# Key buffers by whole head or fixed tile, and the head norm weights applied at the transposed copy, in a streaming encoder step

## The chip, the cores and the metric

One core of a Trainium2 chip runs one launch of the kernel. The metric is the device time of one execution in microseconds (us). The kernel before was timed three times: 1062.08 us in the median, from 1061.17 to 1062.24. The profile is of a separate execution.

## What is computed

The reference is one layer of a hybrid encoder on 1024 prompt rows and 64 sample rows (9 row tiles; the sample rows also see 256 cached rows). Everything is 32-bit floating point.

```python
proj = rms_norm(x) @ w_in                       # 1024 -> 5280 columns
a = softmax(q1 k1) - lam * softmax(q2 k2)       # differential attention, 4 heads
o_a = rms_norm(a @ v, da_head_norm_g) * (1.0 - lam_init)      # per head, 128 wide
o_b = softmax(q_m k_m) @ v_m                    # latent attention (MLA), 8 heads
y = x + (sigmoid(g_a) * ((o_a * silu(z_a)) @ w_branch_a)
         + sigmoid(g_b) * ((o_b * silu(z_b)) @ w_branch_b)) @ w_out
```

Both attentions are causal by chunks of 64 rows. The norm of a differential head is over the 128 columns of the head, so its weight is one number per column, and its factor one number per row.

## The kernel before

A product of two 32-bit operands is made of three matmuls: each operand is split into a rounded part and the rest (`split`, `split_ps`: ScalarE copies, GpSimd or VectorE subtracts), and `mm3` (L252 to L254) multiplies rounded by rounded, rounded by rest and rest by rounded.

The program runs in stages: the projections for the latent attention, then the latent attention (`mla_streams`), then the differential attention (`da_streams`), then the rest of the dense work, the branch products and the output product. Through both attentions a background stream (`dense`) gives TensorE the remaining columns of the input projection, 24 matmuls for one PSUM buffer; I call them dense matmuls. Their results are copied by ScalarE (L904) into `st` tiles (`stg`, 4 buffers) and stored to HBM.

TensorE's order is made by a planner in Python (`Order`): each stream is a generator that yields the time at which its next step can be ready, what it costs on TensorE and which buffers it takes (`Slots`), and the planner always takes the stream that can go on first. The order on the other engines and the order of the DMAs come from the Tile scheduler. PSUM has four one-bank buffers (`pj`), which transposes, attention products and dense work share, and two two-bank buffers for scores (`sc`).

**Latent attention.** `fetch` loads, for each head, keys in chunks of 512, 512 and 320 columns (raw tiles from `rawp`, 4 buffers of 512) and splits each into a tile of its own (`kp`, 4 buffers). `unit` takes one query tile t: scores against `128*(t+1)` keys, in chunks of 512 and the rest (L1004 to L1006), the maximum (VectorE L1012), the exponential (ScalarE L1015), the division by the sum (GpSimd L1017), the transposes (L1035). `out` multiplies by the values (L1073, L1074).

**Differential attention.** A key chunk is loaded by rows, transposed by TensorE (L1178) and written by `put_k` into a tile `K` of four planes: both key halves rounded, and their rests, which are zero in the other half's 64 partitions. GpSimd writes those zeros anew for each of the 12 chunks (L1174, L1175). The scores are L1233 and L1234, the mask L1236, the maximum L1238, the exponential L1240, the transposes L1261, the value products L1276 and L1278; the head's 9 output tiles collect in `oraw` (`H.o`) (L1283, L1284). After the ninth, VectorE works out the factor `fd` of each row (L1292 to L1297; the square root is ScalarE's and needs another function table there and back) and multiplies the 9 tiles by `fd` and the weights `gda`, which lie on all partitions:

```python
for t_ in range(NT):
    m = rows(t_)
    V.scalar_tensor_tensor(H.o[:m, t_], H.o[:m, t_], fd[:m, t_:t_ + 1], gda[:m], op0=ALU.mult, op1=ALU.mult)
```

Then `out` transposes them in groups of 4, 4 and 1 (L1311), ScalarE copies each group to the one tile `otT` (L1313), and a DMA stores it to `oT`, which the next stage loads again.

Of the kernel before, what the change touches and what calls it, by code (L numbers as in the profile page):

```python
# [11 lines left out]
F32 = mybir.dt.float32  # L12
# [8 lines left out]
P = 128  # L21
# [34 lines left out]
    (1, 1, S, 4, 128), (1, 1, S, 4, 128), (1, 1, S, 256), (1, 1, S, 32),  # L56
    (1, 1, SS, 4, 128), (1, 1, SS, 4, 128), (1, 1, SS, 256), (1, 1, SS, 32),
)


def rows(t):
# [3 lines left out]
def f32(ap):  # L65
    return ap.bitcast(F32)
# [105 lines left out]
def trunk(ctx: ExitStack, tc: tile.TileContext, i: dict, o: list):  # L172
# [751 lines left out]


    def mla_streams(fx):
        kp = pool(fx, "kp", 4)
        vp = pool(fx, "vp", 4)
        qp = pool(fx, "qp", 3)
        rawp = pool(fx, "rawp", 4)  # L930
        pcp = pool(fx, "pcp", 4)
        ptp = pool(fx, "ptp", 3)
        otp = pool(fx, "otp", 2)
        s_k, s_v, s_q, s_pc, s_pt = Slots(4), Slots(4), Slots(3), Slots(4), Slots(3)
        start = od.now + 16.0

        class Head:
# [9 lines left out]
        def fetch():  # L947
            for H in heads:
                h = H.h
                pr, e = h // 2, h % 2  # L950
                hs = slice(64 * e, 64 * e + 64)
                for what in (("k", 0), ("q", 0), ("q", 1), ("k", 1), ("q", 2), ("q", 3), ("k", 2), ("q", 4)):
                    c = what[1]
                    if what[0] == "k":
                        yield start, 0.0, [(s_k, 1), (s_v, 1)]
                        k0, n = (0, 512, S)[c], (512, 512, 320)[c]
                        raw = rawp.tile([P, 512], F32, name="raw")
                        load(raw[:MR, :n], mk[h, :, k0:k0 + n])
                        K = kp.tile([MR, 2, 512], F32R, name="K")
                        split(raw[:MR, :n], K[:, 0, :n], K[:, 1, :n])  # L960
                        H.K[c], H.tK[c] = K, t_split(od.on_dma(P * n * 4), n)
                        raw = rawp.tile([P, 512], F32, name="raw")
                        Vt = vp.tile([P, 4, 2, 64], F32R, name="V")
                        nb = 4 if c < 2 else 2
                        rv = raw[:, 0:256].rearrange("p (b d) -> p b d", d=64)
                        load(rv[:, :nb], mv[k0:k0 + nb * P, h * 64:(h + 1) * 64].rearrange("(b p) d -> p b d", p=P))
                        split(rv[:, :nb], Vt[:, :nb, 0], Vt[:, :nb, 1])
                        if c == 2:
                            load(rv[:SS, 2], mv[S + PAST:TK, h * 64:(h + 1) * 64])
                            split(rv[:SS, 2], Vt[:SS, 2, 0], Vt[:SS, 2, 1])  # L970
                        H.V[c], H.tV[c] = Vt, t_split(od.on_dma(130e3), 256)
                    else:
                        yield start, 0.0, [(s_q, 1)]
                        q0, nq = c * 256, 256 if c < 4 else 64
                        raw = rawp.tile([P, 512], F32, name="raw")
                        load(raw[:MR, :nq], mq[h, :, q0:q0 + nq])
                        Q = qp.tile([MR, 2, 256], F32R, name="Q")
                        split(raw[:MR, :nq], Q[:, 0, :nq], Q[:, 1, :nq])
                        H.Q[c], H.tQ[c] = Q, t_split(od.on_dma(P * nq * 4), nq)

        def unit(H, t):
# [2 lines left out]
            a0 = (t % 2) * P  # L984
            if t < 8:
                nk = P * (t + 1)
                chunks = [(c, min(512, nk - 512 * c)) for c in range((nk + 511) // 512)]
                msz = [P] * (t + 1)
            else:
                nk, chunks, msz = 320, [(2, 320)], [P, P, SS]  # L990

            def ready():
                if jc not in H.tQ or any(c not in H.tK for c, _ in chunks):
                    return None
                return max([H.tQ[jc]] + [H.tK[c] for c, _ in chunks])

            yield ready, sum(3 * c_mm(m) for _, m in chunks) + 0.03, [(s_sc, 1), (s_pc, 1)]
            sc = psc.tile([P, 1024], F32, name="sc")
            Q = H.Q[jc]
            for x_, (c, m) in enumerate(chunks):  # L1000
                dst = sc[:n, x_ * 512:x_ * 512 + m]
                qh, ql = Q[:, 0, a0:a0 + n], Q[:, 1, a0:a0 + n]
                kh, kl = H.K[c][:, 0, :m], H.K[c][:, 1, :m]
                TE.matmul(dst, qh, kh, start=True, stop=False)  # L1004
                TE.matmul(dst, qh, kl, start=False, stop=False)
                TE.matmul(dst, ql, kh, start=False, stop=True)  # L1006
            if t % 2 == 1 or t == 8:
                s_q.give(od.now)
            if t in (7, 8):
                s_k.give(od.now, 2 if t == 7 else 1)  # L1010
# [92 lines left out]


    def da_streams(fx):
        kp = pool(fx, "kpd", 4)
        vp = pool(fx, "vpd", 4)
        qp = pool(fx, "qpd", 3)
        rawp = pool(fx, "rawpd", 3)
        pcp = pool(fx, "pcpd", 4)  # L1110
        ptp = pool(fx, "ptpd", 4)
        otp = pool(fx, "otpd", 1)
        orp = pool(fx, "orp", 2)
        gda = orp.tile([P, P], F32, name="gda", bufs=1)
        load(gda, i["da_head_norm_g"][0].partition_broadcast(P))
        s_k, s_v, s_q, s_pc, s_pt, s_or = Slots(4), Slots(4), Slots(3), Slots(2), Slots(4), Slots(2)

        class Head:
            pass

        heads = []
        for h in range(DA_H):
# [22 lines left out]
        def fetch():  # L1145
            for H in heads:
                h = H.h
                for what in (("k", 0), ("q", 0), ("q", 1), ("k", 1), ("q", 2), ("q", 3), ("k", 2), ("q", 4)):
                    c = what[1]
                    if what[0] == "k":  # L1150
# [18 lines left out]
                            split(rv[:SS, 2], Vt[:SS, 2, 0], Vt[:SS, 2, 1])  # L1169
                        H.V[c], H.tV[c] = Vt, t_split(od.on_dma(512e3), 512)  # L1170
                        yield od.dma + 0.95, 0.11 * len(bl), [(s_tr, 1)]
                        K = kp.tile([P, 4, 512], F32R, name="K")

                        G.memset(f32(K[64:128, 2]), 0.0)  # L1174
                        G.memset(f32(K[0:64, 3]), 0.0)  # L1175
                        tr = ptr.tile([P, 512], F32, name="pj")
                        for b, m in enumerate(bl):
                            TE.transpose(tr[:, b * P:b * P + m], rk[:m, b], ident[:m, :m])  # L1178
# [23 lines left out]
        def unit(H, t):  # L1202
# [86 lines left out]
            if H.n == NT:  # L1289
# [222 lines left out]
```

## Time and profile before

| | us |
|---|---|
| median of three runs | 1062.08 |
| the profiled execution | 1064.11 |
| its span, first to last instruction | 1062.3 |
| TensorE busy in the span | 1027.8 |
| VectorE, ScalarE, GpSimd busy | 589.8, 557.3, 317.9 |

PE stands for TensorE's matmuls, PEld for its weight loads, DVE for VectorE, ACT for ScalarE, POOL for GpSimd, SP for SyncE, whose queue issues nearly all DMAs. A wait names the instruction whose end released the engine. Matmuls overlap in the pipeline, so a matmul's price is read from its start to the start of the next, not from its duration. The latent attention stands at about 250 to 518 us, the differential attention at about 530 to 800, the first branch product at 864.6.

### The profile page before, as it was taken

The page shows a single profiled execution, that of the slowest core. Times are in us where ns is not written, and L with a number is a line of the kernel's source. Part 1 is how long each engine was busy: PE and PEld are TensorE (multiplying, and loading weights), DVE is VectorE, ACT ScalarE, POOL GpSimd, SP SyncE. Part 2 cuts the span into 40 slices and gives each one's busy share as a digit, 9 for nine tenths or more (in the row PEclk, how much of TensorE's full clock was granted, in tenths as well). Part 3 has the DMA queues.
Part 4 walks back from the last instruction along what each step waited for, and adds up shares of the span by engine and source line. Part 5 has one row for each costly group of instructions (what it writes and reads, how often), then busy time and mean ns, then how long its engine had stood idle before and what let it go on. Part 6 is the DMA issues. An engine that isn't in the chain of part 4 may idle for free.

```text
span 1062.3 us, 18645 instructions
## 1 busy us (share of the span) xinstructions
PE 1027.8 (97%) x6391; PEld 971.0 (91%) x6391; DVE 589.8 (56%) x1396; ACT 557.3 (52%) x1411; POOL 317.9 (30%) x401
## 2 busy tenths in 40 slices
PE   5989999999999999999999989999999999999997
PEld 5989899999999999999999989899899999998885
DVE  5765833015566656665357767667754513564743
ACT  5554413335666666566456666666656554423422
POOL 3012202015545455444321222122103553512200
PEclk8999999999999999999999999999999999999999
DMA  6443556565323542332243232332218875531322
GB/s 214 125 103 70 130 133 181 177 159 157 100 82 96 138 112 68 95 93 76 74 119 99 60 110 69 98 96 65 74 50 264 255 250 180 171 103 50 110 80 80
DMA packets 154878, 126.64 MB, mean 119 GB/s; under 512 B 36960, under 2 KB 141792, under 8 KB 154784
## 3 DMA queue, kind: packets, MB, share of 16 engines
q1 hardware_dynamic: 153552, 123.22, 40.3%
q10 hardware_dynamic: 1232, 2.23, 0.6%
q8 instruction: 51, 0.84, 0.3%
q14 instruction: 43, 0.35, 0.1%
HBM read 80.50 MB, written 45.52 MB: 119 GB/s over the span
## 4 chain that ended last, share of the span: by engine, by line
PE 45%; DVE 2%; DMA 2%; ACT 2%; issue 1%; SPq 0%; POOL 0%; ACTq 0%
PE pj L252 12%; PE pj L254 11%; PE pj L253 11%; PE pj L1276 2%; PE sc L1233 2%; PE sc L1234 2%; PE pj L1261 2%; DMA oT<-otT 1%; PE pj L1278 1%; DVE oraw L1300 1%; DMA z<-zT 1%; SPq L190 0%; PE pj L1178 0%; PE pj L1196 0%; PE pj L1453 0%
## 5 line engine op out<-in xcount | busy, mean ns | idle before, releaser
L252 PE MATMUL pj<-hT,w 128*128 128x352 f32 (+1 forms) x576 | 199.7, 347 | 4.8 <-DVE ot L1080 1.3
L254 PE MATMUL pj<-hT,w 128*128 128x352 f32 (+1 forms) x576 | 188.3, 327 | 0.0
L253 PE MATMUL pj<-hT,w 128*128 128x352 f32 (+1 forms) x576 | 188.1, 327 | 0.0
L239 POOL TENSOR_TENSOR w<-wr,w 128x384 fp32r<-128x384 f32 (+3 forms) x81 | 74.3, 919 | 280.2 <-ACT w L238 238.8
L252 PE MATMUL pj<-w,hT 128*128 128x384 f32 (+1 forms) x384 | 133.1, 347 | 2.2 <-ACT krt L546 1.0
L253 PE MATMUL pj<-w,hT 128*128 128x384 f32 (+1 forms) x384 | 127.1, 331 | 0.6 <-POOL w L431 0.6
L254 PE MATMUL pj<-w,hT 128*128 128x384 f32 (+1 forms) x384 | 127.0, 331 | 0.3 <-DVE hT L243 0.3
L252 PEld LDWEIGHTS pj<-hT,w 128*128 128x128 f32 x576 | 108.8, 189 | 8.2 <-ACT otT L1313 1.7
L238 ACT ACTIVATE w<-wr 128x384 fp32r<-128x384 f32 (+3 forms) x161 | 73.6, 470 | 68.4 <-PE pj L254 32.4
L253 PEld LDWEIGHTS pj<-hT,w 128*128 128x128 f32 x576 | 108.8, 189 | 0.1
L254 PEld LDWEIGHTS pj<-hT,w 128*128 128x128 f32 x576 | 108.1, 188 | 0.0
L243 DVE TENSOR_TENSOR PT<-pj,PT 128x512 fp32r<-128x512 f32 (+4 forms) x168 | 83.8, 511 | 42.3 <-ACT PT L242 40.8
L239 DVE TENSOR_TENSOR w<-wr,w 128x384 fp32r<-128x384 f32 (+2 forms) x80 | 50.8, 635 | 78.5 <-ACT w L238 78.0
L242 ACT ACTIVATE PT<-pj 128x512 fp32r<-128x512 f32 (+4 forms) x168 | 72.9, 454 | 33.1 <-PE pj L1035 23.0
L252 PEld LDWEIGHTS pj<-w,hT 128*128 128x128 f32 x384 | 73.0, 190 | 4.5 <-ACT krt L546 1.3
L253 PEld LDWEIGHTS pj<-w,hT 128*128 128x128 f32 x384 | 73.1, 190 | 1.4 <-POOL w L431 0.9
L254 PEld LDWEIGHTS pj<-w,hT 128*128 128x128 f32 x384 | 72.7, 189 | 0.6 <-DVE hT L243 0.6
L1017 POOL TENSOR_SCALAR pc<-pc,zs 128x128 f32<-128x128 f32 (+8 forms) x72 | 52.3, 729 | 51.8 <-DVE zs L1016 50.4
L1240 ACT ACTIVATE pc<-sc,mx 128x128 f32<-128x128 f32 (+8 forms) x72 | 51.4, 716 | 28.9 <-DVE mx L1238 28.3
L1012 DVE TENSOR_REDUCE mx<-sc 128x1 f32<-128x128 f32 (+8 forms) x72 | 51.9, 722 | 21.3 <-PE sc L1006 20.4
L254 PE MATMUL pj<-u,w 128*128 128x352 f32 (+1 forms) x192 | 62.8, 327 | 0.0
L253 PE MATMUL pj<-u,w 128*128 128x352 f32 (+1 forms) x192 | 62.8, 327 | 0.0
(252 smaller groups left out, 2524.6 us busy)
## 6 DMA issues: line engine op xcount, KB each, us to landing
wr<-in_w_in SPq DMA_DIRECT2D x84, 192.0 KB
g<-gT SPq DMA_DIRECT2D x16, 544.0 KB
x<-in_x_prompt SPq DMA_DIRECT2D x15, 512.0 KB
dqkv<-st SPq DMA_DIRECT2D x32, 192.0 KB
gT<-st SPq DMA_DIRECT2D x32, 176.0 KB
z<-zT SPq DMA_DIRECT2D x8, 544.0 KB
o<-oT SPq DMA_DIRECT2D x8, 544.0 KB
out<-st SPq DMA_DIRECT2D x64, 64.0 KB
```

Of the source, the lines that this page charges most:

```text
L238: A.activation(hi, raw, AF.Copy)
L239: (eng or G).tensor_tensor(lo, raw, f32(hi), op=ALU.subtract)
L242: A.activation(hi, ps, AF.Copy)
L243: V.tensor_tensor(lo, ps, f32(hi), op=ALU.subtract)
L252: TE.matmul(ps, lh, rh, start=first, stop=False)
L253: TE.matmul(ps, lh, rl, start=False, stop=False)
L254: TE.matmul(ps, ll, rh, start=False, stop=last)
L1012: V.tensor_reduce(out=mx[:n], in_=sc[:n, :nk], op=ALU.max, axis=AX.X, negate=True)
L1017: G.tensor_scalar(pc[:n, :nk], pc[:n, :nk], zs[:n], 1.0, op0=ALU.mult, op1=ALU.mult)
L1233: TE.matmul(dst, qs, H.K[ch][:, c, :m], start=True, stop=False)
L1234: TE.matmul(dst, qs, H.K[ch][:, 2 + c, :m], start=False, stop=not masked)
L1240: A.activation(pc[:n, :nk], sc[:n, :nk], AF.Exp, bias=mx[:n], accum_out=H.z[:n, c, t:t + 1])
```

## The change

Line numbers above 58 are 8 higher after the change from a new function on, and up to 16 higher further down.

Latent attention: a head's 1024 prompt keys lie in one tile (two buffers), the 320 sample keys in another (`Ks`, one buffer). Query tile 4, with 640 keys, is scored in two chunks of 320 in place of 512 and 128; its PSUM columns begin at 192 so that each chunk stays in a bank. The raw tiles are two of 512 columns for keys and three of 256 for queries and values.

Differential attention: the four key tiles are fixed, and their zero parts are written once ahead of the stage, half by VectorE and half by GpSimd. The multiplication by `fd` is one GpSimd instruction for the 8 full tiles and one for the last. The weights are a column of one number per partition and go in as the scale of ScalarE's copy of the transposed output. The groups are 3, 3 and 3 tiles and the copy goes to an `st` tile; `otT` is gone.

```diff
+def key_chunks(nk):
+    if nk <= 512:
+        return [(0, nk)]
+    m = max(nk - 512, 512) if nk != 640 else 320
+    return [(0, m), (m, nk - m)]
...
     def mla_streams(fx):
-        kp = pool(fx, "kp", 4)
+        kp = pool(fx, "kp", 2)
-        rawp = pool(fx, "rawp", 4)
+        rawp = pool(fx, "rawp", 2)
...
-                        K = kp.tile([MR, 2, 512], F32R, name="K")
-                        split(raw[:MR, :n], K[:, 0, :n], K[:, 1, :n])
+                        if c == 0:
+                            H.K[0] = kp.tile([MR, 2, S], F32R, name="K")
+                        elif c == 2:
+                            H.K[1] = kp.tile([MR, 2, 320], F32R, name="Ks", bufs=1)
+                        K = H.K[c // 2][:, :, k0 % S:k0 % S + n]
+                        split(raw[:MR, :n], K[:, 0], K[:, 1])
-                        raw = rawp.tile([P, 512], F32, name="raw")
+                        raw = rawp.tile([P, 256], F32, name="raw2", bufs=3)
...
-                chunks = [(c, min(512, nk - 512 * c)) for c in range((nk + 511) // 512)]
+                ks, chunks, msz = (0, 1)[:(nk + 511) // 512], key_chunks(nk), [P] * (t + 1)
+            b0 = 512 - chunks[0][1] if len(chunks) == 2 else 0
...
-            sc = psc.tile([P, 1024], F32, name="sc")
+            sc = psc.tile([P, 1024], F32, name="sc")[:, b0:]
...
     def da_streams(fx):
-        otp = pool(fx, "otpd", 1)
-        gda = orp.tile([P, P], F32, name="gda", bufs=1)
-        load(gda, i["da_head_norm_g"][0].partition_broadcast(P))
+        gda = orp.tile([P, 1], F32, name="gda", bufs=1)
+        load(gda, i["da_head_norm_g"][0].rearrange("(p a) -> p a", a=1))
+        keys = [kp.tile([P, 4, 512], F32R, name=f"K{e}") for e in range(4)]
+        for K in keys:
+            V.memset(f32(K[64:128, 2]), 0.0)
+            G.memset(f32(K[0:64, 3]), 0.0)
...
-                        K = kp.tile([P, 4, 512], F32R, name="K")
-                        G.memset(f32(K[64:128, 2]), 0.0)
-                        G.memset(f32(K[0:64, 3]), 0.0)
+                        K = keys[(3 * h + c) % 4]
...
-                for t_ in range(NT):
-                    m = rows(t_)
-                    V.scalar_tensor_tensor(H.o[:m, t_], H.o[:m, t_], fd[:m, t_:t_ + 1], gda[:m], op0=ALU.mult, op1=ALU.mult)
-                H.to = od.on_dve(od.on_act(t2, 2500) + 1.0, 2300, 0.001)
+                for m, ts in ((P, slice(0, 8)), (SS, slice(8, 9))):
+                    o_ = H.o[:m, ts]
+                    G.tensor_tensor(o_, o_, fd[:m, ts].unsqueeze(2).broadcast_to(list(o_.shape)), op=ALU.mult)
+                H.to = od.on_pool(od.on_act(t2, 2500) + 2.0, 1152)
...
-            for t0 in (0, 4, 8):
-                ts = range(t0, min(t0 + 4, NT))
+            for t0 in (0, 3, 6):
+                ts = range(t0, t0 + 3)
...
-                ot = otp.tile([P, 512], F32, name="otT")
-                A.activation(ot[:, :w], tr[:, :w], AF.Copy)
+                ot = stg.tile([P, 384], F32, name="st")
+                A.activation(ot[:, :w], tr[:, :w], AF.Copy, scale=gda)
```

The planner's times shift with these lines, so TensorE's order differs from the first 640-key unit on, and with it the other engines' orders. Three places:

VectorE at the end of the first differential head, before, from the reciprocal of the next head's unit to that head's key chunk:

```order
L1249 RECIPROCAL f<-zda 128x1
L1300 SCALAR_TENSOR_TENSOR oraw<-oraw,fd,gda 128x128 x8
L1300 SCALAR_TENSOR_TENSOR oraw<-oraw,fd,gda 64x128
L1250 SCALAR_TENSOR_TENSOR f<-f,zda,neglam 128x1
L1284 TENSOR_TENSOR oraw<-pj,oraw 128x128
L243 TENSOR_TENSOR PT<-pj,PT 128x256
L1238 TENSOR_REDUCE mx<-sc 128x1 x2
L1252 SCALAR_TENSOR_TENSOR pc<-pc,f 128x384
L1133 TENSOR_TENSOR K<-pj,K 64x512
L1134 TENSOR_TENSOR K<-pj,K 64x512
```

The same place now, from the last step of the factor:

```order
L1312 SCALAR_TENSOR_TENSOR fd<-fd,r_7989 128x9
L1253 TENSOR_REDUCE mx<-sc 128x1
L1151 TENSOR_TENSOR K_7007<-pj,K_7007 64x512
L1152 TENSOR_TENSOR K_7007<-pj,K_7007 64x512
L1299 TENSOR_TENSOR oraw<-pj,oraw 128x128
L1253 TENSOR_REDUCE mx<-sc 128x1
L247 TENSOR_TENSOR w<-wr,w 128x256
```

The nine multiplications are gone from this queue, and the next head's key chunk (`K_7007` is the first of the four fixed tiles) stands two instructions behind the factor.

GpSimd between the two attentions, before:

```order
L1017 TENSOR_SCALAR pc<-pc,zs 128x1024
L1174 MEMSET K 64x512
L1175 MEMSET K 64x512
L1174 MEMSET K 64x512
L1175 MEMSET K 64x512
L1174 MEMSET K 64x512
L1175 MEMSET K 64x512
L1174 MEMSET K 64x512
L1175 MEMSET K 64x512
L1017 TENSOR_SCALAR pc<-pc,zs 64x320
```

And now:

```order
L1029 TENSOR_SCALAR pc<-pc,zs 128x896
L1137 MEMSET K_7007 64x512
L1137 MEMSET K_7008 64x512
L1137 MEMSET K_7009 64x512
L1137 MEMSET K_7010 64x512
L247 TENSOR_TENSOR w<-wr,w 128x256
L1029 TENSOR_SCALAR pc<-pc,zs 128x1024
L1029 TENSOR_SCALAR pc<-pc,zs 64x320
```

Four fills of zeros in place of eight stand ahead of the last division, but also ahead of the last but one, and a weight split has come between.

ScalarE at the first differential head's output copies, now:

```order
L1329 ACTIVATE st<-pj,gda 128x384
L1255 ACTIVATE pc,zda<-sc,mx 128x512
L246 ACTIVATE V<-raw 128x2x128
L1329 ACTIVATE st<-pj,gda 128x384
L246 ACTIVATE V<-raw 64x128
L912 ACTIVATE st<-pj 128x384
L1158 ACTIVATE Q<-pj 64x256
L1159 ACTIVATE Q<-pj 64x256
L1329 ACTIVATE st<-pj,gda 128x320
```

The three copies (L1329, before L1313) now share the four `st` buffers with the dense copies (L912, before L904); the value splits that wait for a DMA still stand among them.

## Rows read from the trace of the kernel before

**Rows 1.** The page, parts 1 and 2: busy time; granted clock in 40 slices.

```profile
PE 1027.8 (97%) x6391; PEld 971.0 (91%) x6391; DVE 589.8 (56%) x1396; ACT 557.3 (52%) x1411; POOL 317.9 (30%) x401
...
PEclk8999999999999999999999999999999999999999
```

**Rows 2.** Waits of TensorE, 500 to 830 us: total, times, longest.

```profile
PE pj L1196 <- issue: 1.9, 1, 1.9
PE pj L1035 <- POOL pc L1017: 1.3, 1, 1.3
PE pj L252 <- DVE K L1134: 1.2, 1, 1.2
PE pj L1196 <- ACT otT L1313: 1.2, 1, 1.2
PE pj L252 <- ACT otT L1313: 1.2, 2, 0.8
PE pj L252 <- DVE PT L243: 0.9, 1, 0.9
PE pj L1276 <- ACT otT L1313: 0.6, 1, 0.6
```

**Rows 3.** Timeline of TensorE at a 640-key and a 320-key unit: start, duration, instruction.

```profile
256.92 0.39 PE L1004 MATMUL sc<-K,Q 104*128 104x512 f32 x1
...
257.88 0.39 PE L252 MATMUL pj<-hT,w 128*128 128x384 f32 x1
...
271.69 0.31 PE L1004 MATMUL sc<-K,Q 104*64 104x320 f32 x1
...
272.13 0.32 PE L252 MATMUL pj<-hT,w 128*128 128x352 f32 x1
272.29 0.32 PE L253 MATMUL pj<-hT,w 128*128 128x352 f32 x1
```

**Rows 4.** Timeline of ScalarE at three head ends; in brackets the idle time before.

```profile
622.16 0.22 ACT L1313 ACTIVATE otT<-pj 128x64 f32<-128x64 f32 x1 [2.18 <-DMA oT<-otT]
...
682.12 0.42 ACT L238 ACTIVATE V<-raw 128x256 fp32r<-128x256 f32 x1 [2.58 <-DMA raw<-in_cache_da_v]
...
811.69 1.09 ACT L238 ACTIVATE u<-o 128x1088 fp32r<-128x1088 f32 x1
812.69 0.58 ACT L1313 ACTIVATE otT<-pj 128x512 f32<-128x512 f32 x1
```

**Rows 5.** Timeline of VectorE at the ends of the first and second head.

```profile
606.45 0.17 DVE L1297 SCALAR_TENSOR_TENSOR fd<-fd,r 128x9 f32<-128x9 f32 x1
...
608.03 2.42 DVE L1300 SCALAR_TENSOR_TENSOR oraw<-oraw,fd,gda 128x128 f32<-128x128 f32 x9
...
672.27 4.07 DVE L1300 SCALAR_TENSOR_TENSOR oraw<-oraw,fd,gda 128x128 f32<-128x128 f32 x9
...
677.42 0.69 DVE L1134 TENSOR_TENSOR K<-pj,K 64x512 fp32r<-64x512 f32 x1
```

**Rows 6.** Timeline of GpSimd and VectorE between the attentions.

```profile
511.89 0.52 POOL L1174 MEMSET K<- 64x512 f32 x1
...
515.82 0.52 POOL L1175 MEMSET K<- 64x512 f32 x1
516.33 0.53 POOL L1017 TENSOR_SCALAR pc<-pc,zs 64x320 f32<-64x320 f32 x1
...
516.06 0.43 DVE L1080 TENSOR_TENSOR ot<-pj,ot 64x256 f32<-64x256 f32 x1 [3.77 <-ACT ot L1079]
```

**Rows 7.** Groups by line, GpSimd's product of 1024 columns: busy, mean ns.

```profile
L239 POOL TENSOR_TENSOR ms<-mT,ms 128x1024 fp32r<-128x1024 f32 (+1 forms) x7 | 16.0, 2293 | 55.8 <-ACT ms L238 55.8
```

**Rows 8.** Timeline of TensorE: the first differential head's last value product.

```profile
600.63 0.22 PE L1278 MATMUL pj<-V,PT 64*64 64x128 f32 x1
```

**Rows 9.** Timeline of GpSimd beside VectorE's products of the second head.

```profile
673.39 1.15 POOL L239 TENSOR_TENSOR w<-wr,w 128x384 fp32r<-128x384 f32 x1 [7.11 <-ACT w L238]
674.63 0.62 POOL L1135 TENSOR_SCALAR K<-K 64x512 fp32r<-64x512 f32 x1
```

More of the change, by code (lines that the diff above doesn't have):

```diff
@@ L933, in mla_streams @@
         otp = pool(fx, "otp", 2)
-        s_k, s_v, s_q, s_pc, s_pt = Slots(4), Slots(4), Slots(3), Slots(4), Slots(3)
+        s_k, s_v, s_q, s_pc, s_pt = (Slots(2), Slots(1)), Slots(4), Slots(3), Slots(4), Slots(3)
         start = od.now + 16.0
@@ L954, in fetch @@
                     if what[0] == "k":
-                        yield start, 0.0, [(s_k, 1), (s_v, 1)]
+                        yield start, 0.0, [(s_k[c // 2], 1 - c % 2), (s_v, 1)]
                         k0, n = (0, 512, S)[c], (512, 512, 320)[c]
@@ L958, in fetch @@
                         load(raw[:MR, :n], mk[h, :, k0:k0 + n])
-                        K = kp.tile([MR, 2, 512], F32R, name="K")
-                        split(raw[:MR, :n], K[:, 0, :n], K[:, 1, :n])
-                        H.K[c], H.tK[c] = K, t_split(od.on_dma(P * n * 4), n)
-                        raw = rawp.tile([P, 512], F32, name="raw")
+                        if c == 0:
[4 more added lines that the diff above has]
+                        split(raw[:MR, :n], K[:, 0], K[:, 1])
+                        H.tK[c] = t_split(od.on_dma(P * n * 4), n)
+                        raw = rawp.tile([P, 256], F32, name="raw2", bufs=3)
                         Vt = vp.tile([P, 4, 2, 64], F32R, name="V")
                         nb = 4 if c < 2 else 2
-                        rv = raw[:, 0:256].rearrange("p (b d) -> p b d", d=64)
+                        rv = raw.rearrange("p (b d) -> p b d", d=64)
                         load(rv[:, :nb], mv[k0:k0 + nb * P, h * 64:(h + 1) * 64].rearrange("(b p) d -> p b d", p=P))
@@ L974, in fetch @@
                         q0, nq = c * 256, 256 if c < 4 else 64
-                        raw = rawp.tile([P, 512], F32, name="raw")
+                        raw = rawp.tile([P, 256], F32, name="raw2", bufs=3)
                         load(raw[:MR, :nq], mq[h, :, q0:q0 + nq])
@@ L986, in unit @@
                 nk = P * (t + 1)
-                chunks = [(c, min(512, nk - 512 * c)) for c in range((nk + 511) // 512)]
-                msz = [P] * (t + 1)
-            else:
-                nk, chunks, msz = 320, [(2, 320)], [P, P, SS]
+                ks, chunks, msz = (0, 1)[:(nk + 511) // 512], key_chunks(nk), [P] * (t + 1)
+            else:
+                nk, ks, chunks, msz = 320, (2,), [(0, 320)], [P, P, SS]
+            b0 = 512 - chunks[0][1] if len(chunks) == 2 else 0
             def ready():
-                if jc not in H.tQ or any(c not in H.tK for c, _ in chunks):
+                if jc not in H.tQ or any(c not in H.tK for c in ks):
                     return None
-                return max([H.tQ[jc]] + [H.tK[c] for c, _ in chunks])
+                return max([H.tQ[jc]] + [H.tK[c] for c in ks])
             yield ready, sum(3 * c_mm(m) for _, m in chunks) + 0.03, [(s_sc, 1), (s_pc, 1)]
-            sc = psc.tile([P, 1024], F32, name="sc")
-            Q = H.Q[jc]
-            for x_, (c, m) in enumerate(chunks):
-                dst = sc[:n, x_ * 512:x_ * 512 + m]
+            sc = psc.tile([P, 1024], F32, name="sc")[:, b0:]
+            Q, K = H.Q[jc], H.K[t // 8]
+            for c0, m in chunks:
+                dst = sc[:n, c0:c0 + m]
                 qh, ql = Q[:, 0, a0:a0 + n], Q[:, 1, a0:a0 + n]
-                kh, kl = H.K[c][:, 0, :m], H.K[c][:, 1, :m]
+                kh, kl = K[:, 0, c0:c0 + m], K[:, 1, c0:c0 + m]
                 TE.matmul(dst, qh, kh, start=True, stop=False)
@@ L1009, in unit @@
             if t in (7, 8):
-                s_k.give(od.now, 2 if t == 7 else 1)
+                s_k[t - 7].give(od.now)
             mx = small.tile([P, 1], F32, name="mx")
@@ L1105, in da_streams @@
     def da_streams(fx):
-        kp = pool(fx, "kpd", 4)
+        kp = pool(fx, "kpd", 1)
         vp = pool(fx, "vpd", 4)
```

## The prediction

> **What bounds the kernel now.** I read the page first. [...] There is no idle stretch in which an added matmul would be free, and none in which a removed wait is made up for elsewhere: dense work that TensorE gets done earlier in the attentions is not there any more behind them. A microsecond off TensorE's waits is therefore worth a microsecond of the end. A microsecond on another engine is worth nothing, unless TensorE comes to wait for it.
>
> So I read TensorE's waits next, from the last latent units to the last differential head [rows 2]. There are few, 8.3 us in the rows shown, and nearly all of them stand at four places that the change touches. To see what is behind each I took the timelines of ScalarE [rows 4], VectorE [rows 5] and GpSimd [rows 6] at those places. Durations are of the profiled execution, 1064.11 us, which is 2.03 above the median of the runs, 1062.08. I make the sum against 1064.11 and take the same number of microseconds from the median.
>
> **The change part by part.** *640 keys as 320 and 320.* The number of instructions on TensorE is the same before and after. Only these units change, one for each of 8 heads. With 512 and 128 columns the scores take from 256.92 to 257.88, 0.96 us; a 320-column pair takes from 271.69 to 272.13, 0.44, and two of them 0.88 [rows 3]. The saving is 0.08 x 8, **-0.7** with rounding. It can hardly be more or less, since both prices are start to start on a busy TensorE.
>
> *The output copy in `st`.* `otT` is one buffer, so a group's copy waits until the group before it has been stored: the copy at 622.16 stood idle for 2.18 on that store [rows 4]. TensorE then lacks a PSUM buffer, and that costs it 1.2 + 1.2 + 0.6 = 3.0 [rows 2]. Of this the 0.8 (the longer of the pair) is of another kind: at the last head the copy at 812.69 stood behind a 1.09 us split of `u` [rows 4], which stays. At most 2.2 can go. What is late next on ScalarE are the value splits of the next head, one of which waited 2.58 for its load from the cache [rows 4], and in the new order they still stand between the output copies. I take **-1.6**, between 0 and -2.2, nearer to the full price because the store named in the row is gone as a cause.
>
> *The nine products leave VectorE.* They hold its queue for 2.42 us in the first head and for 4.07 in the second [rows 5]. Queued behind them are the next head's key writes and the addition `PT` that turns into operands of value products. At 678.22 TensorE has a wait of 1.9 that the view calls "issue": the key write that ends at 677.42 + 0.69 = 678.11 [rows 5] is what let it go. With the 0.9 on `PT` and the 1.2 on a key write this makes 4.0 [rows 2]. In the new order the key writes come two instructions behind the factor, and nothing of that length stands ahead of them. GpSimd's own part of the key (0.62 a piece [rows 9]) and the products on GpSimd can still be late, so I take **-3.2**, between 0 and -4.0 and nearer to the full price because the key writes are what the view names.
>
> *The zeros.* Eight fills, from 511.89 to 516.33, 4.4 us, stand ahead of the last division, for which TensorE waits 1.3 [rows 2, 6]. Now four fills and a weight split of 256 columns stand there. A fill is 0.56 with its gap and the split is estimated at 0.8 (two thirds of the 1.15 for 384 columns [rows 9]), so 3.0: the division comes 1.4 earlier. By a count in the two orders TensorE arrives there some seven matmuls earlier too, about 1.1 at 0.16 each (272.13 to 272.29 [rows 3]). So I take **-0.4**, between 0 and -1.3. VectorE's four fills have no row of their own. At GpSimd's price they are 2.1 and fit into the 3.77 us idle stretch that VectorE has at this place [rows 6]; below that price there is nothing to gain, without that cover they would hold `ot` up by at most those 2.1. Inside the differential attention the 16 other fills go from a GpSimd that TensorE was not seen to wait for there; nothing.
>
> *The products arrive at GpSimd.* The chain that the first transpose waits for: the last value product starts at 600.63 [rows 8], the factor is done at 606.45 + 0.17 = 606.62 [rows 5], 6.0 later; then comes the product over 8 x 128 = 1024 columns. A two-operand GpSimd product of that width takes 2.29 in the mean of seven, one other shape among them [rows 7]; it is the nearest row there is, from SBUF to SBUF as here. So `oraw` is ready after 8.3. Between that last value product and the first transpose the new order puts 54 matmuls in the first head, 81, 71 and 57 in the others; at 0.16 each TensorE gets there after 8.6, 13, 11 and 9.1. It should just not wait, with 0.3 to spare in the first head. I take **+0.2**, between 0 and +2 (the whole product coming on top in one head).
>
> [...]
>
> *One ring for two users.* The dense copies and the output copies now share four `st` buffers. A ninth tile's worth of stores is little beside them, but a dense copy may now find the ring taken: **+0.3**; the far end is rival 3.
>
> *At nothing:* whole-head key tiles and smaller raw tiles in the latent attention, where TensorE shows no wait on keys between 500 us and the end of that stage [rows 2], and where the splits of a head come in the same order as before; the one-column load of `gda` (one DMA as before, needed at the first head's end only); the scale in ScalarE's copy, a copy before and a copy after; groups of 3, 3, 3 in place of 4, 4, 1, which is as many transposes and as many stores; the deeper tail behind the attentions, where there is a little less dense work left as cover.
>
> The sum: -0.7 - 1.6 - 3.2 - 0.4 + 0.2 + 0.3 = **-5.4**, 1058.7 for the profiled execution, **1056.7 at the median**. With all the waits gone and nothing added it would be -0.7 - 2.2 - 4.0 - 1.3 = -8.2, 1053.9.
>
> **Rivals.** [...]
>
> *2. The waits only move.* TensorE's order is planned anew, and other waits take the place of those removed, on the value splits above all [rows 4]: a copy that no longer waits for a store waits for ScalarE, and a key that is written early waits for its load. For: the waits on `otT` and on keys already change places from head to head [rows 2]. Against: the waits name causes that are gone. Only the scores count then: -0.7, 1061.4.
>
> *3. Slower: the `st` ring.* A copy that finds no free `st` buffer stops ScalarE's whole queue, exponentials and value splits included, for as long as a store is on its way, as `otT` did with 2.18 [rows 4]. TensorE paid up to 1.2 for such a stop [rows 2]. Without terms 2 and 6 the sum is -4.1; six such stops, two in each of three heads, make 7.2 and the time +3.1, 1065.2. It decides from the sixth stop on (over 4.1 + 2.1). For: in the first head the three output copies come with a dense copy between them. Against: four buffers, where one did with three waits.
>
> **How the numbers follow.** The forecast has 0.70: its two large terms rest on waits whose releasers the rows name. Rival 1 has 0.12, rival 2 0.10, rival 3 0.08. About 0.2%, 2.1 us, is what a measurement of this kernel can tell from no change. Of the forecast's 0.70 I leave 0.03 for a sum smaller than that; rival 1 lies on the bound and is halved. So faster 0.67 + 0.06 = 0.73, same 0.03 + 0.06 + 0.10 = 0.19, slower 0.08. The range goes from 1053.9, all waits gone, to 1061.4, rival 2; outside lie rival 3 and a few hundredths of the forecast.
>
> **What would show it.** In the profile after, the 640-key units should take 0.88 from the first score to the next instruction, no wait of TensorE should name an output copy behind a store, and VectorE should write the next head's keys within 2 us of the factor. The product on GpSimd should take about 2.3 and end before the first transpose of `oraw` starts. TensorE's wait for the last division should be under 1. I am wrong if TensorE waits for GpSimd's `oraw`, if ScalarE waits for a store of `st` at the head ends, or if as many microseconds of waits as before stand at the same places under other names.

## The result, and the profile after

The change makes the kernel slower: 1069.18 us in the median of six executions (1066.85 to 1074.17), against 1062.32 before; the ratio is 1.0068, 95% interval 1.0049 to 1.0086. The forecast was 1056.7 and the range ended at 1061.4.

The trace after is of the execution that took 1066.85, the shortest of the six; that of before took 1064.11, longer than any of its timed runs (1063.91 at most). So the two traces are 2.7 us apart where the medians are 6.9 apart, and they can place only a part of the loss. These 2.7 us have to be found first. The page after, parts 1 and 2:

```profile
PE 1030.7 (97%) x6391; PEld 971.6 (91%) x6391; DVE 585.9 (55%) x1364; ACT 558.6 (52%) x1411; POOL 317.9 (30%) x389
...
PEclk8999999999999999999999999999999998999999
```

TensorE is 2.9 us busier than before [rows 1] with the same 6391 matmuls, and one slice late in the program has a lower clock. TensorE's waits after, 200 to 960 us (total, times, longest):

```profile
PE pj L1047 <- DVE ot L1092: 3.4, 3, 1.5
PE pj L260 <- DVE mT L1435: 3.0, 1, 3.0
PE pj L260 <- ACT st L912: 1.1, 1, 1.1
PE pj L260 <- DVE ot L1092: 0.9, 1, 0.9
...
PE pj L260 <- DVE PT L251: 0.4, 1, 0.4
PE pj L1326 <- ACT st L1329: 0.4, 1, 0.4
PE pj L260 <- DVE K L1152: 0.4, 1, 0.4
PE pj L260 <- ACT st L1329: 0.3, 1, 0.3
```

Against [rows 2] the waits that the forecast spoke of are indeed gone or small: 0.7 in all on output copies where 3.0 stood, no 1.9 on the key write, 0.4 on a key where 1.2 stood, and none on GpSimd's last division where 1.3 stood. Two kinds of wait have come instead: three on `ot` in the latent attention (L1047), and 3.0 on `mT` in the branch products, far behind the last line of the diff. The scores are as forecast: timeline of TensorE, a 640-key unit now, 0.88 from its first matmul to the next instruction.

```profile
255.48 0.31 PE L1016 MATMUL sc<-K,Q 104*128 104x320 f32 x1
...
256.36 0.34 PE L260 MATMUL pj<-hT,w 128*128 128x384 f32 x1
```

So is GpSimd's norm product: the timelines of VectorE and GpSimd after, first head, show it 2.25 us long for both instructions, 1.90 of them for the 1024 columns (forecast 2.29 for these), and the key write 2.2 after the factor's end, with nothing long between.

```profile
616.68 0.17 DVE L1312 SCALAR_TENSOR_TENSOR fd<-fd,r 128x9 f32<-128x9 f32 x1
...
619.06 0.68 DVE L1151 TENSOR_TENSOR K<-pj,K 64x512 fp32r<-64x512 f32 x1 [1.11 <-ACT K L1150]
```

```profile
616.99 2.25 POOL L1315 TENSOR_TENSOR oraw<-oraw,fd 128x1024 f32<-128x1024 f32 x2 [6.14 <-DVE fd L1312]
```

**Where the loss stands.** I cut both traces at the first and at the last dense matmul (counted are those of the `z` and gate columns, `pj<-hT,w`, the first of which starts at 179.0 before and at 177.0 after). From the first to the last it is 685.4 us before and 684.2 after; from the last dense matmul to the last matmul 190.2 before and 196.3 after. (The execution after also began its dense work 2.0 us sooner.) The 6.1 are in the branch products. TensorE there, after:

```profile
878.51 0.66 PE L260 MATMUL pj<-u,w 128*128 128x352 f32 x1 [3.02 <-DVE mT L1435]
878.96 0.50 PE L261 MATMUL pj<-u,w 128*128 128x352 f32 x1
879.26 0.50 PE L262 MATMUL pj<-u,w 128*128 128x352 f32 x1
...
884.78 0.32 PE L260 MATMUL pj<-u,w 128*128 128x352 f32 x1
```

A wait of 3.0, and behind it 6 us of matmuls that start 0.30 apart where 0.16 is usual [rows 3]: the granted clock is down. By stretches of 10 us (PE, PEld, DVE, ACT, POOL busy, then the clock) it stands at 0.89 and 0.77. The 21 matmuls from 878.51 to 884.78 take 6.3 us in place of 3.4 (21 x 0.16), so the slow clock costs an estimated 2.9 more:

```profile
870.00:880.00 10.00, 6.98 (x39) 6.66 (x38) 1.89 (x4) 4.41 (x9) 6.09 (x8) 0.89 0.72 217
880.00:890.00 10.00, 10.00 (x50) 10.00 (x49) 3.96 (x7) 5.69 (x11) 6.72 (x8) 0.77 0.79 234
```

What is late? `mT` of the second product stands in VectorE's queue behind a weight split that waits for ScalarE's part of the split, which stands in ScalarE's queue behind splits of `w_out`, which wait for loads into `st`, which wait on SP for stores out of `st`. Timelines of VectorE, ScalarE and SP after, and SP's wait for the stores, 860 to 876 us:

```profile
877.42 0.56 DVE L247 TENSOR_TENSOR w<-wr,w 128x384 fp32r<-128x384 f32 x1 [9.43 <-ACT w L246]
877.90 1.41 DVE L1435 TENSOR_TENSOR mT<-pj,g 128x384 f32<-128x384 f32 x3
```

```profile
869.25 0.53 ACT L246 ACTIVATE wo<-st 128x384 fp32r<-128x384 f32 x1 [3.13 <-DMA st<-in_w_out]
...
875.93 1.05 ACT L246 ACTIVATE wo<-st 128x384 fp32r<-128x384 f32 x2 [2.83 <-DMA st<-in_w_out]
876.88 0.71 ACT L246 ACTIVATE w<-wr 128x384 fp32r<-128x384 f32 x2
```

```profile
862.76 0.86 SPq L202 DMA_DIRECT2D gT<-st  x2
...
864.24 4.20 SPq L198 DMA_DIRECT2D st<-in_w_out  x2
868.53 0.38 SPq L202 DMA_DIRECT2D gT<-st  x1
```

```profile
SPq L198 <- DMA gT<-st: 3.9, 2, 3.3
```

Before, the order of these three queues is nearly the same, and that ScalarE split runs at 871.58, 5.3 us sooner on each trace's own clock:

```profile
871.58 0.71 ACT L238 ACTIVATE w<-wr 128x384 fp32r<-128x384 f32 x2
```

The whole chain of loads behind the attentions (`z`, `o`, gates, `w_out`) is later against TensorE's work. It begins with the first load of `z`, issued when the differential attention's buffers come free, at 800.67 before and at 805.68 after:

```profile
800.67 2.88 SPq L190 DMA_DIRECT2D z<-zT  x1
```

```profile
805.68 2.90 SPq L198 DMA_DIRECT2D z<-zT  x1
```

With the dense work 2.0 earlier, that is 7 us later; against the last dense matmul the first load of `z` stands 63.8 us ahead before and 55.5 after. TensorE was not slower until there, it had done other work: the order leaves 276 dense matmuls behind the last transposes of `oraw`, where 330 were left before; 54 of them at 0.16 are 9 us of cover.

### The profile page after: what moved, and what is told of

It is laid out like the page before. It is cut to its first block, busy times and chain, and to the rows that moved or that the text cites. A ratio compares the mean times of both kernels' runs of the same rounds, so it can differ in the third digit from the quotient of the medians.

```text
span 1065.1 us, 18578 instructions
## 1 busy us (share of the span) xinstructions
PE 1030.7 (97%) x6391; PEld 971.6 (91%) x6391; DVE 585.9 (55%) x1364; ACT 558.6 (52%) x1411; POOL 317.9 (30%) x389
## 4 chain that ended last, share of the span: by engine, by line
PE 77%; DMA 5%; DVE 4%; ACT 3%; issue 2%; POOL 1%; SPq 1%; DVEq 0%; ACTq 0%; POOLq 0%
PE pj L260 19%; PE pj L262 18%; PE pj L261 18%; PE pj L1047 3%; PE pj L1291 2%; PE pj L1086 2%; PE sc L1248 2%; PE pj L1085 2%; PE sc L1249 2%; PE pj L1276 2%; PE sc L1016 2%; PE sc L1017 2%; PE sc L1018 2%; DMA o<-oT 2%; PE pj L1293 1%
## 5 line engine op out<-in xcount | busy, mean ns | idle before, releaser
L247 DVE TENSOR_TENSOR w<-wr,w 128x384 fp32r<-128x384 f32 (+2 forms) x80 | 55.1, 690 | 80.7 <-ACT w L246 80.2
L1027 ACT ACTIVATE pc<-sc,mx 128x128 f32<-128x128 f32 (+8 forms) x72 | 51.6, 717 | 31.2 <-DVE mx L1024 30.8
L260 PE MATMUL pj<-u,w 128*128 128x352 f32 (+1 forms) x192 | 64.1, 334 | 3.0 <-DVE mT L1435 3.0
L1255 ACT ACTIVATE pc<-sc,mx 128x128 f32<-128x128 f32 (+8 forms) x72 | 51.4, 715 | 26.5 <-DVE mx L1253 26.0
```

The costliest lines, as they stand in the source:

```text
L247: (eng or G).tensor_tensor(lo, raw, f32(hi), op=ALU.subtract)
L260: TE.matmul(ps, lh, rh, start=first, stop=False)
L1027: A.activation(pc[:n, :nk], sc[:n, :nk], AF.Exp, bias=mx[:n], accum_out=zs[:n])
L1255: A.activation(pc[:n, :nk], sc[:n, :nk], AF.Exp, bias=mx[:n], accum_out=H.z[:n, c, t:t + 1])
```

## The experiments

Theory 1 came out of this: the new order gives TensorE's dense work out sooner, ends the attentions later and leaves the load chain uncovered. Its rival, theory 2, was the changed attention code itself. Later I split theory 1 by what tips the order; theory 1a says that the order alone makes the loss, whatever the instructions. Of each run the table has the dense matmuls left (counted in the order), the time from the first to the last dense matmul and from there to the last matmul (start to start in its one trace), and the median of its executions with the ratio to the kernel before, which was timed again beside each set of runs. A trace is of one execution, and those of one kernel lie up to 7.7 us apart (w_out_later, 1062.32 to 1070.01), so single microseconds of the two stretches are not the medians'.

| run | left | dense, us | rest, us | median, us | ratio, interval |
|---|---|---|---|---|---|
| before | 330 | 685.4 | 190.2 | 1062.3 | |
| the change | 276 | 684.2 | 196.3 | 1069.2 | 1.0068 (1.0049 to 1.0086) |
| scores_512_128 | 348 | 680.4 | 190.2 | 1059.3 | 0.9971 (0.9960 to 0.9981) |
| da_of_before | 258 | 690.6 | 192.9 | 1070.1 | 1.0072 (1.0055 to 1.0088) |
| otT_back | 318 | 692.9 | 190.2 | 1072.7 | 1.0097 (1.0084 to 1.0110) |
| w_out_later | 276 | 685.7 | 194.3 | 1064.7 | 1.0028 (1.0014 to 1.0042) |
| new_scores_old_plan | 348 | 679.5 | 190.2 | 1057.9 | 0.9962 (0.9950 to 0.9974) |
| old_scores_new_plan | 276 | 686.4 | 196.0 | 1070.5 | 1.0071 (1.0056 to 1.0086) |
| old_plan_norm_on_dve | 348 | 689.2 | 190.2 | 1067.5 | 1.0052 (1.0040 to 1.0064) |
| old_plan_otT | 348 | 681.3 | 190.2 | 1059.8 | 0.9979 (0.9970 to 0.9988) |
| before_told_088 | 258 | 687.4 | 190.7 | 1068.3 | 1.0065 (1.0052 to 1.0078) |
| told_110 | 276 | 681.3 | 196.6 | 1067.4 | 1.0059 (1.0043 to 1.0074) |
| told_080 | 363 | 683.3 | 190.2 | 1063.0 | 1.0011 (0.9999 to 1.0022) |
| old_plan_w_out_later | 348 | 678.8 | 190.2 | 1058.4 | 0.9968 (0.9956 to 0.9980) |

**scores_512_128**, the change with

```diff
-    m = max(nk - 512, 512) if nk != 640 else 320
+    m = 512
```

> The change with one thing undone: query tile 4 is scored in 512 and 128 columns again. The scores alone cost 0.7 us more. But TensorE's order is planned anew and leaves 348 dense matmuls behind the last transposes of the differential attention, where the change leaves 276 and the kernel before 330. Theory 1 (lost cover: the loss of the change stands in the first branch products, because the loads of z, o, gates and w_out have 54 matmuls, 9 us, less work in front of them): no wait of 3 us in the first branch products and none of the slow clock behind it, median 1059.5 to 1062. Theory 2 (the changed attention code itself, GpSimd's product and the shared st ring, makes the time long and uneven): 1068 to 1071.

1059.3, 0.2 under theory 1's range. The smallest part of the change, undone, turns 7 us of loss into 3 us of gain, and the wait of 3.0 and the slow clock are gone: 190.2 for the rest.

**da_of_before**, the whole of `da_streams` of the kernel before in the changed kernel:

```diff
     def da_streams(fx):
-        kp = pool(fx, "kpd", 1)
+        kp = pool(fx, "kpd", 4)
...
-                    G.tensor_tensor(o_, o_, fd[:m, ts].unsqueeze(2).broadcast_to(list(o_.shape)), op=ALU.mult)
+                    V.scalar_tensor_tensor(H.o[:m, t_], H.o[:m, t_], fd[:m, t_:t_ + 1], gda[:m], op0=ALU.mult, op1=ALU.mult)
...
```

> The latent attention of the change with the whole differential attention of the kernel before (nine products on VectorE, otT, zeros written per chunk). The order leaves 258 dense matmuls behind the last transposes, 18 fewer than the change. Theory 1 (lost cover): at least as slow as the change, 1069 to 1075, with the wait in the branch products of 3 us or more. Theory 2 (changed attention code): back near the kernel before, 1061 to 1063.

1070.1: the attention code that the rival blames is gone and the loss is not. But the wait in the branch products is smaller than theory 1 said (1.7 and 0.5) and most of the loss is in the dense stretch, 690.6. So lost cover is not the whole of what an order does.

**otT_back**, the change with the `otT` pool, its copy and the groups of before:

```diff
-            for t0 in (0, 3, 6):
-                ts = range(t0, t0 + 3)
+            for t0 in (0, 4, 8):
+                ts = range(t0, min(t0 + 4, NT))
...
-                ot = stg.tile([P, 384], F32, name="st")
+                ot = otp.tile([P, 512], F32, name="otT")
...
```

> The change with the single otT buffer and the groups of 4, 4 and 1 back; norm product, weights and zeros as changed. 318 dense matmuls are left behind the last transposes, 12 fewer than before. Theory 1 (lost cover): most of the loss is gone, 1060 to 1064. Theory 2 (changed attention code): if the shared st ring is what costs, 1062; if GpSimd's product is, 1069.

1072.7, a miss for both theories. TensorE's longest waits there, and ScalarE's timeline at the first of them:

```profile
PE pj L260 <- ACT otT L1329: 3.6, 1, 3.6
PE pj L1047 <- DVE ot L1092: 3.4, 3, 1.5
PE pj L260 <- DVE Q L1162: 2.8, 1, 2.8
```

```profile
817.11 1.11 ACT L246 ACTIVATE u<-o 128x1088 fp32r<-128x1088 f32 x1 [3.62 <-DVE o L1400]
818.12 1.09 ACT L1399 ACTIVATE z<-z 128x1088 f32<-128x1088 f32 x1
819.12 0.67 ACT L1329 ACTIVATE otT<-pj,gda 128x512 f32<-128x512 f32 x1
```

The copy named `otT` stands behind a split of `u`, and that one waits for `o`, the load chain again, before the last dense matmul this time. It is the kind of wait that cost 0.8 before [rows 2, 4]. The three waits on `ot` are those of the change.

**w_out_later**, the change with the `w_out` parts behind the fifth to eighth gate:

```diff
-            if br == 1 and j % 2 == 1:
-                load_wo(j // 2)
+            if br == 1 and j >= 4:
+                load_wo(j - 4)
...
-            split(raw[:, :n], wo[k][:, 0, c0:c0 + n], wo[k][:, 1, c0:c0 + n], G)
+            tc.keep_in_program_order(A.activation(wo[k][:, 0, c0:c0 + n], raw[:, :n], AF.Copy))
+            G.tensor_tensor(wo[k][:, 1, c0:c0 + n], raw[:, :n], f32(wo[k][:, 0, c0:c0 + n]), op=ALU.subtract)
```

> The change, and the first four parts of w_out are loaded and split behind the fifth to eighth gate sigmoid in place of the second, fourth, sixth and eighth, so that ScalarE has the weight splits of the fourth and fifth branch product ahead of them. TensorE's order is the change's, 276 dense matmuls left. Theory 1, with the path st store, w_out load, w_out split, weight split, VectorE's weight split, mT, PSUM: the wait of 3 us goes or falls under 1 and the median is 1061 to 1064. If the loads of o, z and gates are late whatever stands behind them, the wait stays at the same branch product and the median is 1067 to 1071.

1064.7: with the same order of TensorE, 4.5 us of the loss went with the `w_out` splits, just above the range given. The wait on `mT` is gone. Its trace, of the longest of its nine executions (1070.01), has 2.4 at the first branch product instead, on a dense copy that stands behind a gate and a `u` split, which waited 3.1 for `o`. The link through `w_out` is shown; the lateness behind it stays, at least in that execution.

**new_scores_old_plan** and **old_scores_new_plan** part the scoring from the order. What the planner is told for a unit is changed. The diff is the first's; the second has the scores in 512 and 128 columns and `[320, 320]` in the planner's list:

```diff
-            yield ready, sum(3 * c_mm(m) for _, m in chunks) + 0.03,
+            yield ready, sum(3 * c_mm(m) for m in ([512, 128] if len(chunks) == 2 and nk == 640 else [m for _, m in chunks])) + 0.03,
```

> The change, with the scores in two chunks of 320, but the planner is told the TensorE time of 512 and 128 columns for the 640-key units (1.04 us by its own formula in place of 0.88). TensorE's order becomes that of the run with 512 and 128, 348 dense matmuls left behind the last transposes, while the scoring is the change's. Theory 1a (it is the order alone, tipped by a cost that fell by 0.16 us in 8 units): 0.7 under that run's 1059.3, so 1058 to 1059. Rival (the scoring in two halves itself costs, by its place in PSUM or by what it does to the reader of the maximum): 1066 to 1070.

> The reverse: the scores in 512 and 128 columns, but the planner is told the time of two chunks of 320, so that TensorE's order is the change's, 276 dense matmuls left. Theory 1a (order alone): 1068 to 1072, with the four waits on ot in the latent attention and the wait in the branch products as in the change. Rival (the scoring itself): 1058 to 1061.

1057.9 and 1070.5. The order is the loss: TensorE's matmuls stand in the order of scores_512_128 in the first trace and in the order of the change in the second, one by one. The scoring in two halves costs nothing. In both orders it comes out shorter (1057.9 against 1059.3, 1069.2 against 1070.5), but the intervals overlap, so a gain of 1.4 or 1.3 is not clear of the noise. Waits of TensorE 200 to 960 us, the three largest in the first and the four largest in the second:

```profile
PE pj L260 <- ACT st L912: 1.1, 1, 1.1
PE pj L260 <- DVE ot L1092: 0.9, 1, 0.9
PE pj L1047 <- DVE PT L251: 0.8, 1, 0.8
```

```profile
PE pj L1047 <- DVE ot L1092: 3.4, 3, 1.5
PE pj L260 <- DVE mT L1435: 2.5, 1, 2.5
PE pj L260 <- ACT st L912: 2.3, 2, 1.2
PE pj L1326 <- ACT st L912: 1.4, 1, 1.4
```

The second has the change's waits, on `ot` and on `mT`, though not its scores.

**old_plan_norm_on_dve**, with the planner's line of the first of these, puts the nine products back (the weights again on all partitions):

```diff
-                for m, ts in ((P, slice(0, 8)), (SS, slice(8, 9))):
-                    o_ = H.o[:m, ts]
-                    G.tensor_tensor(o_, o_, fd[:m, ts].unsqueeze(2).broadcast_to(list(o_.shape)), op=ALU.mult)
+                for t_ in range(NT):
+                    m = rows(t_)
+                    V.scalar_tensor_tensor(H.o[:m, t_], H.o[:m, t_], fd[:m, t_:t_ + 1], gda[:m], op0=ALU.mult, op1=ALU.mult)
...
-                A.activation(ot[:, :w], tr[:, :w], AF.Copy, scale=gda)
+                A.activation(ot[:, :w], tr[:, :w], AF.Copy)
...
```

> As the first run of this set (scores in 320s, planner told 512 and 128), with the head norm back on VectorE: nine products with fd and the weights on all partitions, the output copy without a scale. The planner is told nothing of it, so TensorE's order is the same and only the engine of the norm differs. By the forecast's terms 3 and 5 (3.2 for VectorE's queue, 0.2 for GpSimd's chain) 3.0 more than the first run, 1061 to 1062; if no operand that TensorE needs stands behind the nine products in this order, the same as the first run within 0.7.

1067.5: 9.6 more than with GpSimd, three times what terms 3 and 5 said. VectorE's nine products in the four heads, TensorE's waits, and TensorE's busy time and clock (the number behind POOL's) behind the second and the third head:

```profile
606.86 2.43 DVE L1315 SCALAR_TENSOR_TENSOR oraw<-oraw,fd,gda 128x128 f32<-128x128 f32 x9
...
668.85 4.06 DVE L1315 SCALAR_TENSOR_TENSOR oraw<-oraw,fd,gda 128x128 f32<-128x128 f32 x9
...
737.11 4.09 DVE L1315 SCALAR_TENSOR_TENSOR oraw<-oraw,fd,gda 128x128 f32<-128x128 f32 x9
741.13 0.54 DVE L1253 TENSOR_REDUCE mx<-sc 128x1 f32<-128x384 f32 x1
...
805.14 2.44 DVE L1315 SCALAR_TENSOR_TENSOR oraw<-oraw,fd,gda 128x128 f32<-128x128 f32 x9
```

```profile
PE sc L1248 <- ACT pc L1255: 4.4, 2, 2.8
PE pj L1276 <- DVE pc L1267: 2.2, 1, 2.2
```

```profile
676.00:684.00 8.00, 8.00 (x42) 7.70 (x40) 4.11 (x10) 4.09 (x12) 1.38 (x2) 0.79 0.40 125
...
744.00:752.00 8.00, 6.01 (x23) 5.90 (x24) 4.43 (x11) 3.58 (x9) 0.73 (x1) 0.57 0.20 58
```

The waits between 520 and 830 us are 9.1 in sum against 3.1 with GpSimd, 6.0 more. The lower clock costs an estimated 8.00 x 0.21 = 1.7 behind the second head and, in the 6.01 us in which TensorE was busy, 6.01 x 0.43 = 2.6 behind the third. Together that is 10.3; the dense stretch is 9.7 longer (689.2 against 679.5). The longest wait, 2.8 on `pc` of the exponential, came from VectorE: the maximum that the exponential needs ran at 741.13, right behind the nine products of the third head.

**old_plan_otT**, the first with the single `otT` buffer (groups of 3 kept):

```diff
-                ot = stg.tile([P, 384], F32, name="st")
+                ot = otp.tile([P, 512], F32, name="otT")
...
```

> As the first run of this set, with the output copy back in one otT buffer (groups of 3, 3 and 3 kept, st used by the dense copies alone). Same order of TensorE. By the forecast's terms 2 and 6 (1.6 and 0.3) 1.3 more than the first run, 1059.5 to 1060.5; if the store of a single buffer lets ScalarE stand as it did in the kernel with otT back (3.6 us on TensorE at the last head, and the clock after it), 3 to 6 more, 1062 to 1065.

1059.8, 1.9 more: term 2 with term 6, forecast at 1.3. The intervals of the two runs overlap a little (0.9970 to 0.9988 and 0.9950 to 0.9974), so the sign is likely and the size is not clear.

The last four are of the order alone. **before_told_088**, **told_110** and **told_080** change one number that the planner is told, the first in the kernel before, the others in the change (1.10, 0.80):

```diff
-            yield ready, sum(3 * c_mm(m) for _, m in chunks) + 0.03,
+            yield ready, (0.88 if nk == 640 else sum(3 * c_mm(m) for _, m in chunks)) + 0.03,
```

> The kernel before, with nothing changed but the number that the planner is told for a 640-key unit of the latent attention: 0.88 us, as the change tells it, in place of 1.04. No instruction is added, removed or resized; the order leaves 258 dense matmuls behind the last transposes, as in the run with the differential attention of before. Theory 1a (the order alone makes the loss): 1067 to 1073. If the new code is needed for it: 1061 to 1063.

1068.3. The kernel before loses 6 us by a number that no instruction contains. Its trace (of its shortest execution, 1066.67) has 2.0 us more than before in the dense stretch and 0.5 behind it, so most of the 6 us can't be placed. The two longest waits of TensorE are 2.4 where 1.3 stood [rows 2] and 2.2 where there was none:

```profile
PE pj L1035 <- POOL pc L1017: 2.4, 1, 2.4
PE pj L1035 <- DVE PT L243: 2.2, 1, 2.2
```

This run also limits what the order alone explains. TensorE's matmuls stand here in the order of da_of_before, and up to the end of the latent attention in that of the change. Yet the three waits on `ot` are not here, while da_of_before has them:

```profile
PE pj L1047 <- DVE ot L1092: 3.4, 3, 1.5
```

So these 3.4 us come of the order together with the new latent code. Lost cover alone is not enough either: with 258 dense matmuls left, the first load of `z` stands 51.5 us ahead of the last dense matmul, less than the 55.5 of the change, and still TensorE has no wait in the branch products. The ScalarE split that the change waited for comes 12.0 us behind the last dense matmul (866.57) here:

```profile
878.52 0.71 ACT L238 ACTIVATE w<-wr 128x384 fp32r<-128x384 f32 x2
```

In the change it comes 15.7 behind, and 3.0 of them were too much. Why the loads of `w_out` took longer there stays open.

> The change, with the planner told 1.10 us for a 640-key unit, 0.06 more than the 1.04 that gave 1057.9. The order tips back: 276 dense matmuls are left behind the last transposes. Theory 1a with lost cover: 1066 to 1072. If the time goes with how truly the planner's number is told, and not with what order comes out of it: 1057 to 1060.

> The change, with the planner told 0.80 us for a 640-key unit, 0.08 less than the change tells it. The order leaves 363 dense matmuls behind the last transposes, 15 more than the best run so far. Theory 1a with lost cover: no wait in the branch products, 1056.5 to 1061, the rest open by what waits this order has in the attentions. If the count left is not what matters: 1066 or more.

1067.4 and 1063.0. The first is as expected: 0.06 on the other side of the good number and the change is slow again, with 196.6 behind the last dense matmul. The second has no wait in the branch products, as expected, but a median 2 above the range: its order has other waits in the attentions (1.9 ahead of a query's transposes, 1.7 on an output copy). In told_110 the wait of the branch products is 3.6 on a dense copy, not on `mT`. The count left is a sign for the branch products, not a rule (190.2 in all runs with 318 or more, 194.3 to 196.6 with 276, but 190.7 and 192.9 with 258), and it doesn't tell the time.

**old_plan_w_out_later**, both edits together:

```diff
+            yield ready, sum(3 * c_mm(m) for m in ([512, 128] if len(chunks) == 2 and nk == 640 else [m for _, m in chunks])) + 0.03,
...
+            if br == 1 and j >= 4:
+                load_wo(j - 4)
...
```

> The scores of the change with the old plan (1057.9) and w_out loaded later, as in the run that gave 1064.7. If the late w_out only takes away a wait that the change's order has, it brings nothing here: 1057 to 1059. If it is a gain of its own of 4.5 us: 1053 to 1054.

1058.4, as without it (1057.9). The later `w_out` was worth 4.5 only where the loads were late.

## Why the prediction was wrong

**What failed** is the entry at the end of "At nothing": "the deeper tail behind the attentions, where there is a little less dense work left as cover". It measured 6.1 us, 196.3 for 190.2, with 54 dense matmuls fewer behind the transposes. In the dense stretch, to which all terms of the sum belong, the traces give a gain of 1.2 where 5.4 was forecast. The sum has no term for waits that a new order brings, and those in the latent attention (200 to 520 us) came to 4.9 where 2.8 stood, the 1.3 on the last division [rows 2], 0.2 on `ot` and this one:

```profile
PE pj L252 <- DVE ot L1080: 1.3, 1, 1.3
```

With the entry falls "A microsecond off TensorE's waits is therefore worth a microsecond of the end". The sentence ahead of it, that dense work done earlier is not there any more behind the attentions, is also why it can be missed there as cover. I took the new order as given and costed the edits within it. But the edit that I gave 0.7 us also changed the planner's figure for 8 units, from 1.04 to 0.88, and with it the planner's later choices. The matmuls left could have been counted in the order before any run.

That the order makes the loss is shown by new_scores_old_plan, old_scores_new_plan and before_told_088, and the path through the `w_out` loads by w_out_later. What in an order costs how much stays open: before_told_088 leaves less cover than the change and loses 0.5 in the branch products.

**How much each half weighs.** Against the run with the same instructions and the other order (new_scores_old_plan), the change's trace loses 684.2 - 679.5 = 4.7 in the dense stretch and 6.1 behind it. Of the 4.7, the waits in the latent attention make 2.9 (4.9 against 2.0); the rest is not placed. In the medians it is 11.3.

**The sum came near, in part by luck.** With the old plan the same edits give 1057.9, 4.2 under the 1062.2 that the kernel before took beside it; the forecast was -5.4. Term by term, in that order: the scores -0.7, measured -1.4 (not clear of the noise); terms 2 and 6 together -1.3, measured -1.9; terms 3 and 5 together -3.0, measured -9.6, since there the next exponential waits for VectorE as well (2.8 us), and the clock falls (to 0.79 and 0.57 over 8 us). Together these make 12.9 and not 4.2. They are not parts of the 4.2, as the orders of the two kernels differ, so a total that comes near does not bear out its terms. Term 4 was not run alone; the wait on the last division, 1.3 before, is not there in that run.

**The rivals.** Rival 1, that GpSimd holds up the head's end, is refuted: its product took 2.25 us, and TensorE had no wait on it. GpSimd was quicker than the nine instructions of VectorE [rows 5], by 0.2 or by 1.8 a head. That this rival would lie on the bound of 2.1 us was my estimate, and no run shows the longer product that it needs. Rival 3 named the right sign and the wrong place: the `st` ring does stop SP's queue (3.9 us), and ScalarE behind it (3.13 and 2.83 us among others), but at the `w_out` loads, where the change left it as it was. Rival 2 had it that waits move; they moved out of the stage that I watched, and to a higher price than its 1061.4.

## What to carry to other kernels

Where a planner writes the order, an edit's cost model is part of the edit: change the code and keep the number, or the number and keep the code, before the time is put down to either. Count in the new order how much filler is left for the next stage, and look when that stage's loads start against it. The count is a warning and no price: 276 left cost 6.1 here and 258 cost 0.5 in before_told_088.

## What the runs showed of the hardware

VectorE's nine products took 2.43 and 2.44 us in the first and the fourth head of old_plan_norm_on_dve, where GpSimd ran no split beside them, and 4.06 and 4.09 in the second and the third, where it did, as in [rows 5, 9]. Beside 2.37 and 2.26 us of GpSimd instructions, a weight split and two key pieces each time, the nine took 1.6 longer. The direction agrees in four of four heads; by what the nine become longer is not shown.

With a wait of 3.0 us 6.1 were lost: in the trace after, the granted clock stood at 1.00 ahead of the wait (870 to 876 us) and at 0.50 behind it (878.5 to 884), and matmuls started 0.30 apart for 6 us. In the latent attention of the same trace, with waits up to 1.5, the clock stays at 1.00. In old_plan_norm_on_dve TensorE was busy for 4.94 of the 8 us from 668 to 676 and for 4.99 of the 8 us from 736 to 744, and over the 8 us behind each the clock stood at 0.79 and at 0.57. From what wait on the clock falls is not shown.
